# Eight minima over a row of zeros behind each tile, on VectorE, in a fused residual add and RMS norm

## The chip, the cores and the metric

The kernel runs on one core of a Trainium2 chip. The metric is the device time of one execution in microseconds (us). A ratio is the mean time of one kernel's runs over the mean of the other's runs of the same rounds, so it is not quite the ratio of the medians that are quoted.

## The reference

```python
z = x + residual                                   # 32 x 2048 x 2048, float32
rms = np.sqrt(np.mean(z ** 2, axis=-1, keepdims=True) + eps)
return (z / rms * gamma).astype(np.float32)
```

It reads 1074 MB and writes 537 MB.

## The kernel before

The 65536 rows are cut into 74 tiles, of 128 partitions times 7 rows but for the first two. Two buffers `z` hold x, then the sum, then the result. One area `r_area` of 11 rows holds the residual, with four rows to spare, so that a new residual can land while half of the old one is still read. SyncE issues the x loads and the stores on one queue, ScalarE issues the residual loads, but for the first two, on another.

```python
def sp_turn(sp, t):                      # SyncE, one tile
    t.wait(sp, "done", -1)
    # ... store of tile i-1, from z[(i-1) % 2]
    t.wait(sp, "s_out", -1)              # the store has landed: that z is free
    # ... load of x for tile i+1 into it (for the last tile in four parts)

def dve_turn(v, t, own):                 # VectorE, one tile
    t.wait(v, "x_in"); t.wait(v, "r_in")
    (a0, b0), (a1, b1) = parts(i)
    inc(add(v, i, a0, b0), "add_a", i)
    inc(add(v, i, a1, b1), "add_b", i)
    for h, (a, b) in enumerate(parts(i)):
        t.wait(v, "rms_a" if h == 0 else "rms_b")
        v.reciprocal(...)
        ins = scale(v, i, a, b, rstd[p][h])
    inc(ins, "done", i)

# ScalarE: waits for add_a, issues the residual load of tile i+1,
# then sums the squares of each half and takes the root
```

Of the kernel before, what the change touches and what calls it, by code (L numbers as in the profile page):

```python
# [9 lines left out]
def kernel(  # L10
# [5 lines left out]
    eps: float,  # L16
    out: bass.AP,
):



# [7 lines left out]
    P = nc.NUM_PARTITIONS  # L29
# [20 lines left out]
    last = n_tiles - 1  # L50

    LO = 3
# [12 lines left out]
    def sb(name, shape):  # L65
        return ctx.enter_context(nc.sbuf_tensor(name, shape, fp32))
# [6 lines left out]
    def sem(name):  # L73
        sems.append(ctx.enter_context(nc.semaphore(name)))
        return sems[-1]
# [6 lines left out]
    ssq = [[sb(f"ssq{p}{h}", [P, 4]) for h in range(2)] for p in range(2)]  # L82
    rms = [[sb(f"rms{p}{h}", [P, 4]) for h in range(2)] for p in range(2)]
    rstd = [[sb(f"rstd{p}{h}", [P, 4]) for h in range(2)] for p in range(2)]
    tail_ssq = sb("tail_ssq", [P, R])
    tail_rms = sb("tail_rms", [P, R])
    tail_rstd = sb("tail_rstd", [P, R])
# [8 lines left out]
    dve = sem("dve_own")  # L96
    act = sem("act_own")
    s_tail = sem("s_tail")
    tail_ev = {k: sem(f"tail_{k}") for k in ("add", "rms", "done")}


# [7 lines left out]
    def parts(i):  # L109
        if i == 0:  # L110
            return [(0, 2), (2, sizes[0])]
        k = sizes[i] if i < 2 else R
        return [(STEP, k), (0, STEP)] if i % 2 else [(0, R - STEP), (R - STEP, R)]
# [15 lines left out]
    def inc(ins, kind, i):  # L129
        return ins.then_inc(ev[kind][i % 2], U)  # L130
# [38 lines left out]
    def add(v, i, a, b):  # L169
        e = entry(i)  # L170
        s = z[i % 2][:, a:b, :]
        return v.tensor_add(out=s, in0=s, in1=r_area[:, e + a : e + b, :])  # L172

    def scale(v, i, a, b, rs, c=0):
        for g in range(a, b):
            s = z[i % 2][:, g, :]
            ins = v.scalar_tensor_tensor(  # L177
                out=s,
                in0=s,
                scalar=rs[:, c + g - a : c + g - a + 1],  # L180
                in1=gamma_tile[:, :],
                op0=mult,
                op1=mult,
            )
        return ins

    def dve_turn(v, t, own):
        i, p = t.i, t.p
        t.wait(v, "x_in")
        t.wait(v, "r_in")  # L190
# [4 lines that stand above are left out]
            n = b - a  # L195
            t.wait(v, "rms_a" if h == 0 else "rms_b")
            v.reciprocal(out=rstd[p][h][:, :n], in_=rms[p][h][:, :n]).then_inc(dve, U)  # L197
            v.wait_ge(dve, own(i, h))
            ins = scale(v, i, a, b, rstd[p][h])
        inc(ins, "done", i)  # L200


    class Chain:
# [69 lines left out]
    def vector_program(v):  # L273
        v.memset(eps_tile[:, :], float(eps))  # L274
        v.memset(stage, 0.0).then_inc(tail_ev["add"], 1)  # L275
        v.wait_ge(g_in, 4 * U)
        v.stream_shuffle(gamma_tile[:, :].rearrange("p (a b) -> p a b", a=16), stage, [0] * 32)  # L277
        for i in range(LO):
            dve_turn(v, Turn(i), lambda i, h: (2 * i + h + 1) * U)
        with v.Fori(0, 2 * n_iter, 2) as it:  # L280
            for i in range(LO, LO + 2):
                dve_turn(v, Turn(i, it), lambda i, h: it * (2 * U) + (2 * i + h + 1) * U)
        for i in range(HI, last):
            dve_turn(v, Turn(i), lambda i, h: (2 * i + h + 1) * U)
        base = 2 * last * U
        t = Turn(last)
        t.wait(v, "r_in")

        def tail_scale(k):
            a, b = tail[k]  # L290
            v.wait_ge(tail_ev["rms"], k + 1)
            v.reciprocal(out=tail_rstd[:, a:b], in_=tail_rms[:, a:b]).then_inc(dve, U)  # L292
            v.wait_ge(dve, base + (k + 1) * U)
            scale(v, last, a, b, tail_rstd, a).then_inc(tail_ev["done"], 1)

        for k, (a, b) in enumerate(tail):
            v.wait_ge(x_tail[k], U)
            add(v, last, a, b).then_inc(tail_ev["add"], 1)
            if k:
                tail_scale(k - 1)  # L300
        tail_scale(len(tail) - 1)
# [21 lines left out]

    sync_program(nc.sync)
    vector_program(nc.vector)
    scalar_program(nc.scalar)

# [40 lines left out]
```

## Time and profile before

| what | before |
|---|---|
| time, median of 3 | 3724.92 us |
| period of one tile | 50.8 us, 22.02 MB |
| transfers | 433 GB/s over the span |
| VectorE busy | 62% |
| VectorE waits for x | 1252.5 us, 17.6 us a tile |
| first add of the last tile waits for x | 5.6 us |

### The profile page before, as it was taken

The numbers are of one execution on the slowest core, as the hardware profiler recorded it, in microseconds if no ns is written. First come the engines' busy times: TensorE is split into PE (matmuls) and PEld (weight loads), VectorE is DVE, ScalarE is ACT, GpSimd is POOL, SyncE is SP. The second block draws the span as 40 slices with busy tenths as digits, with TensorE's granted clock in tenths as the row PEclk, the third lists the DMA queues.
The fourth block names the chain that finished last, engine by engine and source line by source line (L and its number), as shares of the span: only waits on it lengthen the run. The fifth ranks groups of instructions, "written<-read, shape, count | busy, mean of one in ns | idle before, by whom it ended". The sixth has DMA issues, their size and how long they took to land.

```text
span 3723.7 us, 3798 instructions
## 1 busy us (share of the span) xinstructions
DVE 2302.6 (62%) x816; ACT 1072.4 (29%) x1176; POOL 0.2 (0%) x4
## 2 busy tenths in 40 slices
DVE  5666665566665566665566665566665566665566
ACT  2233322233322233322233322233322233322233
POOL 0000000000000000000000000000000000000000
DMA  9999999999999999999999999999999999999999
GB/s 421 431 434 435 434 434 435 434 435 435 434 434 434 434 434 434 434 434 433 434 434 434 434 434 434 434 434 434 434 434 434 434 434 434 434 434 434 434 432 398
DMA packets 32963, 1610.68 MB, mean 433 GB/s; under 512 B 3712, under 2 KB 3776, under 8 KB 3776
## 3 DMA queue, kind: packets, MB, share of 16 engines
q1 hardware_dynamic: 22592, 1082.17, 67.2%
q10 hardware_dynamic: 10368, 528.49, 32.8%
q14 instruction: 3, 0.02, 0.0%
HBM read 1073.77 MB, written 536.87 MB: 433 GB/s over the span
## 4 chain that ended last, share of the span: by engine, by line
DMA 67%; DVE 22%; issue 9%; ACT 2%; SPq 0%; DVEq 0%; ACTq 0%
DMA out_dram<-z 39%; DMA z<-in_x_dram 27%; DVE z L172 15%; DVE z L177 7%; ACT sq_junk L223 1%; ACT rms L231 0%; DVE rstd L197 0%; SPq L259 0%; DVEq L127 0%; DVE r_area L275 0%; ACTq L211 0%; ACTq L127 0%; SPq L141 0%; DVE tail_rstd L292 0%; SPq L162 0%
## 5 line engine op out<-in xcount | busy, mean ns | idle before, releaser
L172 DVE TENSOR_TENSOR z<-z,r_area 128x8192 f32<-128x8192 f32 (+2 forms) x150 | 1109.5, 7437 | 1252.5 <-DMA z<-in_x_dram 1252.5
L223 ACT ACTIVATE sq_junk<-z 128x2048 f32<-128x2048 f32 x512 | 963.4, 1882 | 2617.1 <-DVE z L172 2605.7
L177 DVE SCALAR_TENSOR_TENSOR z<-z,rstd,gamma_tile 128x2048 f32<-128x2048 f32 x505 | 1153.6, 2344 | 5.2
L197 DVE RECIPROCAL rstd<-rms 128x4 f32<-128x4 f32 (+2 forms) x146 | 25.3, 173 | 130.8 <-ACT rms L231 130.8
L223 ACT ACTIVATION_READ_ACCUMULATOR sq_junk<-z 128x1 f32 x512 | 95.5, 186 | 0.0
L231 ACT ACTIVATE rms<-ssq,eps_tile 128x4 f32<-128x4 f32 (+2 forms) x146 | 43.3, 297 | 13.4
L177 DVE SCALAR_TENSOR_TENSOR z<-z,tail_rstd,gamma_tile 128x2048 f32<-128x2048 f32 x7 | 16.2, 2345 | 0.1
L277 DVE LOAD_MASK_SELECT gamma_tile<-r_area x1 | 0.0, 14 | 16.1 <-DMA r_area<-in_gamma_dram 16.1
L277 DVE STREAM_SHUFFLE gamma_tile<-r_area 128x2048 f32<-128x2048 f32 x1 | 2.3, 2290 | 0.0
L275 DVE MEMSET r_area<- 128x2048 f32 x1 | 1.8, 1765 | 0.4 <-issue 0.4
L223 ACT ACT_TABLE_LOAD x1 | 1.3, 1283 | 0.9 <-SPq L77 0.9
L231 ACT ACT_TABLE_LOAD x1 | 1.3, 1283 | 0.1
L231 ACT ACTIVATE tail_rms<-tail_ssq,eps_tile 128x2 f32<-128x2 f32 (+1 forms) x4 | 1.2, 295 | 0.1
L274 DVE MEMSET eps_tile<- 128x1 f32 x1 | 0.1, 59 | 1.0 <-SPq L77 1.0
L292 DVE RECIPROCAL tail_rstd<-tail_rms 128x2 f32<-128x2 f32 (+1 forms) x4 | 0.6, 158 | 0.0
L349 POOL MEMSET const-bfloat16-1.0<- 128x1 bf16 x1 | 0.1, 101 | 0.0
L349 POOL MEMSET const-uint8-127<- 128x1 uint8 x1 | 0.1, 101 | 0.0
L349 POOL MEMSET const-float32-0.0<- 128x1 f32 x1 | 0.1, 98 | 0.2 <-issue 0.2
L349 POOL MEMSET const-float32-1.0<- 128x1 f32 x1 | 0.1, 98 | 0.0
## 6 DMA issues: line engine op xcount, KB each, us to landing
r_area<-in_residual_dram ACTq DMA_DIRECT2D x72, 7168.0 KB, 35.5
z<-in_x_dram SPq DMA_DIRECT2D x71, 7168.0 KB, 27.5
out_dram<-z SPq DMA_DIRECT2D x71, 7168.0 KB, 40.8
z<-in_x_dram SPq DMA_DIRECT2D x3, 2048.0 KB, 17.9
out_dram<-z SPq DMA_DIRECT2D x3, 2048.0 KB, 15.0
r_area<-in_residual_dram SPq DMA_DIRECT2D x1, 5120.0 KB, 25.0
z<-in_x_dram SPq DMA_DIRECT2D x1, 5120.0 KB, 36.7
out_dram<-z SPq DMA_DIRECT2D x1, 5120.0 KB, 26.5
```

The source lines that it names most:

```text
L172: return v.tensor_add(out=s, in0=s, in1=r_area[:, e + a : e + b, :])
L177: ins = v.scalar_tensor_tensor(out=s, in0=s, scalar=rs[:, c + g - a : c + g - a + 1], in1=gamma_tile[:, :], op0=mult, op1=mult,)
L197: v.reciprocal(out=rstd[p][h][:, :n], in_=rms[p][h][:, :n]).then_inc(dve, U)
L223: s.activation(out=sq_junk[:, :], in_=src[:, g, :], func=Act.Square, accum_out=sq[:, g - a : g - a + 1],)
L231: return s.activation(out=rm, in_=sq[:, : b - a], func=Act.Sqrt, bias=eps_tile[:, :], scale=inv_d)
L274: v.memset(eps_tile[:, :], float(eps))
L275: v.memset(stage, 0.0).then_inc(tail_ev["add"], 1)
L277: v.stream_shuffle(gamma_tile[:, :].rearrange("p (a b) -> p a b", a=16), stage, [0] * 32)
L292: v.reciprocal(out=tail_rstd[:, a:b], in_=tail_rms[:, a:b]).then_inc(dve, U)
L349: nc = _bacc.Bacc("TRN2", target_bir_lowering=False, num_devices=1)
```

## The change

It adds VectorE work that nobody uses, behind the last scaling of each of the tiles 3 to 72, where VectorE would wait for the next x. No other engine's program changes. The intent is to see whether work in a wait costs anything.

```diff
+    zeros = sb("zeros", [P, 1536])
+    least = sb("least", [P, 8])
...
+    spare = sem("spare")
...  in dve_turn
         inc(ins, "done", i)
+        if i >= LO:
+            v.wait_ge(spare, i - LO + 1 if t.it is None else t.it + (i - LO + 1))
+            v.tensor_reduce(
+                out=least[:, :],
+                in_=zeros[:, :].unsqueeze(1).to_broadcast([P, 8, 1536]),
+                op=mybir.AluOpType.min,
+                axis=mybir.AxisListType.X,
+            ).then_inc(spare, 1)
...  in vector_program
         v.memset(stage, 0.0).then_inc(tail_ev["add"], 1)
+        v.memset(zeros[:, :], 0.0).then_inc(spare, 1)
         v.wait_ge(g_in, 4 * U)
...  ahead of the last tile
+        v.wait_ge(spare, last - LO + 1)
```

## The prediction

> **What bounds the kernel now.** I read the page from the top: engine shares, the slices, then the chain that ended last, then the waits, then one period of the timeline, and last the tail. First the page:
>
> ```profile
> span 3723.7 us, 3798 instructions
> DVE 2302.6 (62%) x816; ACT 1072.4 (29%) x1176; POOL 0.2 (0%) x4
> ...
> GB/s 421 431 434 435 434 434 435 434 435 435 434 434 434 434 434 434 434 434 433 434 434 434 434 434 434 434 434 434 434 434 434 434 434 434 434 434 434 434 432 398
> ...
> DMA 67%; DVE 22%; issue 9%; ACT 2%; SPq 0%; DVEq 0%; ACTq 0%
> ```
>
> VectorE is busy 62% of the span, and the transfers run at 433 to 435 GB/s in every slice but the first two and the last two. 1610.68 MB at 434 GB/s take 3711 us of the 3724: the kernel is bound by its transfers. Next, who waits for whom:
>
> ```profile
> ACT sq_junk L223 <- DVE z L172: 2605.7, 149, 35.3
> DVE z L172 <- DMA z<-in_x_dram: 1252.5, 74, 18.7
> DVE rstd L197 <- ACT rms L231: 130.8, 73, 6.2
> ```
>
> VectorE's big wait is for x. Asked for 150 to 3650 us alone, the same view gives 1216.8 us in 69 waits, 17.63 us each. The timeline shows where each lies:
>
> ```profile
> 1858.63 15.16 DVE L172 TENSOR_TENSOR z<-z,r_area 128x6144 f32<-128x6144 f32 x2 [17.63 <-DMA z<-in_x_dram]
> ...
> 1882.69 9.12 DVE L177 SCALAR_TENSOR_TENSOR z<-z,rstd,gamma_tile 128x2048 f32<-128x2048 f32 x4
> 1891.84 0.34 SPq L153 DMA_DIRECT2D out_dram<-z  x1
> 1909.43 15.16 DVE L172 TENSOR_TENSOR z<-z,r_area 128x6144 f32<-128x6144 f32 x2 [17.62 <-DMA z<-in_x_dram]
> ```
>
> One period is 1909.43 - 1858.63 = 50.80 us, and it moves three blocks of 7.34 MB (x, residual, out), 22.02 MB: 433 GB/s, so the period is the transfers' time. VectorE's work on a tile runs from 1858.63 to 1891.81 = 33.2 us; then it issues nothing until x lands. That gap is the room the change has. It is stable: in the timelines I read of the steady stretch it is 17.61 to 18.00 us, and 18.73 after tile 3, the first tile that gets the new work.
>
> The last tile is different, because its x comes in four parts:
>
> ```profile
> 3661.65 9.12 DVE L177 SCALAR_TENSOR_TENSOR z<-z,rstd,gamma_tile 128x2048 f32<-128x2048 f32 x4
> ...
> 3676.41 4.43 DVE L172 TENSOR_TENSOR z<-z,r_area 128x4096 f32<-128x4096 f32 x1 [5.63 <-DMA z<-in_x_dram]
> ...
> 3681.24 4.43 DVE L172 TENSOR_TENSOR z<-z,r_area 128x4096 f32<-128x4096 f32 x1 [0.40 <-DMA z<-in_x_dram]
> ...
> 3690.41 18.76 SPq L269 DMA_DIRECT2D out_dram<-z  x4
> ```
>
> Here the gap is 5.63 us, not 17.6, and from 3681 to 3708.8 VectorE works nearly without a pause. The last store is issued at 3708.84 and lands 13.8 us later by the list of transfers, about 1 us before the end.
>
> **What the Trainium skill says.** Four places.
> - "VectorE: DVE Perf Modes", section "The perf-mode tier table (the rule you actually need)": `tensor_reduce` runs at 1x in every dtype, one element per cycle, as fp32 `tensor_tensor` does, for which it gives 2293 ns at 2048 elements. The trace has 2287 ns for the add of that size, so the table fits for the add; no reduce is in this trace.
> - The same page, "Rules for kernel authors", calls `tensor_reduce` the slowest DVE op and says to expect 1x. Nothing here tests it; it is why I keep a rival with a slower reduce.
> - "SBUF — State Buffer", section "Who interferes with whom": transfers have ports of their own and never contend with a compute engine. The trace agrees (columns: stretch, length, busy VectorE, ScalarE and GpSimd, clock, transfer share, GB/s):
>
> ```profile
> 1841.00:1858.60 17.60, 0.00 (x0) 0.00 (x0) 0.00 (x0) 1.00 0.99 427
> 1858.60:1873.80 15.20, 15.17 (x3) 6.30 (x7) 0.00 (x0) 1.00 1.02 441
> 1873.80:1881.00 7.20, 6.94 (x4) 7.03 (x7) 0.00 (x0) 1.00 1.03 446
> ```
>
>   With VectorE idle the transfers move 427 GB/s, with it fully busy 441 and 446. Busy VectorE costs them nothing visible.
> - "DMA: Bandwidth & Descriptors", section "Where 436 GB/s comes from": the fabric in front of SBUF carries 435.2 GB/s. The slices show 433 to 435, so this kernel is at that ceiling, with no rate left to win or to catch up with.
>
> **The change, part by part.** It removes nothing.
>
> 1. One memset of 128x1536 zeros before the gamma shuffle. The memset of 128x2048 took 1765 ns, so about 1765 x 1536/2048 = 1.3 us. Right after it VectorE waits 16.07 us for gamma; hidden, 0 us. The memset whose end releases the gamma load still comes first.
>
> 2. In the loop over tiles 3 to 72, one reduce behind each tile: 70 of them, each one instruction over 8 x 1536 = 12288 elements. Its duration from the adds: 128x8192 takes 8685 ns, 128x4096 takes 4421 ns; the slope is 4264/4096 = 1.041 ns per element and the fixed part 8685 - 8192 x 1.041 = 157 ns. So 12288 x 1.041 + 157 = 12.95 us (estimate). All 70: 906 us more of VectorE, from 2302.6 to about 3210 us, 86% of the span.
>
> 3. Where it lies. The order of VectorE's instructions in the built program has the reduce behind the last scaling of a tile and ahead of the next tile's first add. The store of the tile is released by the scaling, which is ahead of the reduce, so it is issued as before. The reduce then starts at once and ends 12.95 us into a gap of 17.63 us; 17.63 - 12.95 = 4.7 us of wait remain. The add starts when x lands, as before. Cost per tile: 0, for 69 of the 70. The waits for x should fall by 69 x 12.95 = 894 us.
>
> 4. The wait on the new semaphore is for the reduce of one tile earlier, 50 us past; it and the register operation that goes with it cost some tens of ns inside the gap: 0.
>
> 5. The 70th reduce meets the short gap. It starts at 3670.8 and ends at 3683.75, so the first add of the last tile starts 7.4 us late. The second add would have started at 3681.24 and starts at about 3688.2: 7.0 us late, as 0.4 us of wait are used up. Everything after follows on VectorE without slack, so the four last stores are issued 7.0 us later, the last at 3715.8 instead of 3708.84. How much of 7.0 us reaches the end depends on the transfers still queued. In the kernel before they run near full rate until 3715 although the last store was issued at 3708.84: its 13.8 us to land are mostly queueing, since 1.05 MB take 2.4 us at 434 GB/s. After the change, the third store (2.1 MB) is issued at about 3713.3 to an almost empty queue. Its bytes and the last store's, 3.15 MB, take 7.3 us; for start and landing I take 2.9 us, which is what the first x load leaves (10.1 us for 3.15 MB, some of it shared): landing at 3713.3 + 7.3 + 2.9 = 3723.5, against 3722.6 before. So about +1 us, and surely less than +7; I take +2.5 us, as my queue model is crude.
>
> Sum: 0 + 0 + 69 x 0 + 2.5 = 2.5 us on 3724.9, giving **3727.5 us**.
>
> **The rivals.**
>
> A. The reduce is slower than an element per cycle. The room is 17.63 us, that is 36% over my estimate, or 1.42 ns per element. At two cycles per element it lasts 25.75 us, overruns by 8.1 us, and VectorE becomes the bound: 33.2 + 25.75 = 59 us a tile against 50.8, 70 x 8.1 = 570 us more, near 4295 us. For it: no reduce in this trace, the skill's remark on the slowest op, and an input with step 0 over the eight repeats. Against it: the tier table, and the inner 1536 elements are contiguous. I give it 6%.
>
> B. VectorE's reads slow the transfers. At even 2% less rate in the 12.95 us per tile this would cost 70 x 0.26 = 18 us. Against it: 427 GB/s idle and 441 busy, above. Under 3%.
>
> C. The busy share as the bound: adding 906 us to VectorE in full would give 4631 us. Against it: the gap in front of each first add ends with x, not with VectorE. Nearly excluded.
>
> D. The tail hands on its whole 7 us: 3732 us. Possible if the stores' landing doesn't shrink; still within 2%.
>
> E. A gain from reordered transfers: no store or load is issued earlier, so none. Under 1%.
>
> **Range and chances.** Between no loss and D lie 3724 and 3732 us; a little spare on both sides for chip noise (the three runs differ by 0.2 us) and for weak contention gives 3722 to 3738. Faster by over 2%: 0.01. Slower by over 2% needs more than 74 us, that is over 1 us a tile, which only A does: 0.07. Within 2%: 0.92.
>
> **What would show it.** Right: 70 reduces of about 12950 ns; VectorE near 3210 us and 86%; its wait for x down from 1252.5 to about 350 us, some 4.7 us a tile; period still 50.8 us; slices still at 434 GB/s; in the tail no wait ahead of the first add, the last store issued near 3715.8 and landing in about 8 us. Wrong: a reduce of over 17.6 us with no wait for x left (A), slices under 430 GB/s with waits left over (B), or a last store that still takes 13.8 us to land (D).

## The result, and the profile after

The changed kernel takes 3725.21 us (median of 4 runs, 3724.81 to 3725.66) against 3724.94 us of the kernel before (4 runs, 3724.76 to 3725.41). The ratio is 1.0001, 95% interval 0.9983 to 1.0018: the same time, with 906 us more work.

From the page of the changed kernel: the span, engine shares, GB/s by slice and the new group (line, engine, operation, output and input, count, then busy us, mean ns, idle before).

```profile
span 3723.9 us, 3939 instructions
DVE 3204.3 (86%) x887; ACT 1072.4 (29%) x1176; POOL 0.2 (0%) x4
...
GB/s 421 431 433 434 434 434 434 434 434 434 436 434 434 434 434 434 434 434 434 434 434 435 434 434 434 434 434 434 434 434 434 434 434 434 434 434 434 434 433 398
...
L207 DVE TENSOR_REDUCE least<-zeros 128x8 f32<-128x12288 f32 x70 | 906.3, 12947 | 0.0
```

VectorE went from 62% to 86% of the span and the slices did not move. The busy share alone tells nothing of the time. Who waited for whom in the changed kernel (total us, times, longest):

```profile
ACT sq_junk L235 <- DVE z L176: 2613.0, 148, 34.9
DVE z L176 <- DMA z<-in_x_dram: 359.0, 72, 13.4
DVE rstd L201 <- ACT rms L243: 130.8, 73, 6.2
```

Only the middle line changed, from 1252.5 to 359.0 us: the new work was taken out of the wait for x, 893.5 us of it, while ScalarE's waits are those of before. The timeline of the same stretch as before (start, duration):

```profile
1841.36 12.95 DVE L207 TENSOR_REDUCE least<-zeros 128x8 f32<-128x12288 f32 x1
1859.23 15.16 DVE L176 TENSOR_TENSOR z<-z,r_area 128x6144 f32<-128x6144 f32 x2 [4.92 <-DMA z<-in_x_dram]
...
1892.33 12.95 DVE L207 TENSOR_REDUCE least<-zeros 128x8 f32<-128x12288 f32 x1
1910.05 15.16 DVE L176 TENSOR_TENSOR z<-z,r_area 128x6144 f32<-128x6144 f32 x2 [4.77 <-DMA z<-in_x_dram]
```

The reduce starts as soon as the tile's scaling ends and is over 4.8 us before x lands; from add to add it is still 50.82 us. The tail of the changed kernel:

```profile
3670.80 12.95 DVE L207 TENSOR_REDUCE least<-zeros 128x8 f32<-128x12288 f32 x1
3683.79 8.76 DVE L176 TENSOR_TENSOR z<-z,r_area 128x4096 f32<-128x4096 f32 x2
...
3697.61 18.76 SPq L281 DMA_DIRECT2D out_dram<-z  x4
```

Here the reduce overran the short gap: the first add has no wait in front of it and starts at 3683.79 instead of 3676.41, and the last four stores are issued 7.2 us later (3697.61 against 3690.41 for the first). Yet the end moved by 0.2 us. The list of transfers (the last store, KB, us from issue to landing) says why; first the kernel before,

```profile
out_dram<-z SPq DMA_DIRECT2D x1, 1024.0 KB, 13.8
```

then the changed kernel:

```profile
out_dram<-z SPq DMA_DIRECT2D x1, 1024.0 KB, 6.7
```

The store is issued 7 us later and lands 7 us sooner after its issue: in the kernel before it had stood in a queue.

### The profile page after: what moved, and what is told of

Same layout as the page of the kernel before. It is cut to its first block, busy times and chain, and to the rows that moved or that the text cites. A ratio compares the mean times of both kernels' runs of the same rounds, so it can differ in the third digit from the quotient of the medians.

```text
span 3723.9 us, 3939 instructions
## 1 busy us (share of the span) xinstructions
DVE 3204.3 (86%) x887; ACT 1072.4 (29%) x1176; POOL 0.2 (0%) x4
## 4 chain that ended last, share of the span: by engine, by line
DMA 66%; DVE 23%; issue 9%; ACT 2%; DVEq 0%; SPq 0%; ACTq 0%
DMA out_dram<-z 39%; DMA z<-in_x_dram 27%; DVE z L176 15%; DVE z L181 7%; ACT sq_junk L235 2%; DMA r_area<-in_gamma_dram 0%; DVE least L207 0%; ACT rms L243 0%; DVE rstd L201 0%; DVEq L293 0%; DVEq L131 0%; SPq L271 0%; DVE r_area L287 0%; ACTq L223 0%; ACTq L131 0%
## 5 line engine op out<-in xcount | busy, mean ns | idle before, releaser
L176 DVE TENSOR_TENSOR z<-z,r_area 128x8192 f32<-128x8192 f32 (+2 forms) x150 | 1109.3, 7437 | 359.1 <-DMA z<-in_x_dram 359.0
L181 DVE SCALAR_TENSOR_TENSOR z<-z,rstd,gamma_tile 128x2048 f32<-128x2048 f32 x505 | 1153.6, 2344 | 5.2
L207 DVE TENSOR_REDUCE least<-zeros 128x8 f32<-128x12288 f32 x70 | 906.3, 12947 | 0.0
L201 DVE RECIPROCAL rstd<-rms 128x4 f32<-128x4 f32 (+2 forms) x146 | 25.3, 173 | 130.8 <-ACT rms L243 130.8
## 6 DMA issues: line engine op xcount, KB each, us to landing
z<-in_x_dram SPq DMA_DIRECT2D x71, 7168.0 KB, 27.5
out_dram<-z SPq DMA_DIRECT2D x71, 7168.0 KB, 40.8
```

What stands on the lines that cost most here:

```text
L176: return v.tensor_add(out=s, in0=s, in1=r_area[:, e + a : e + b, :])
L181: ins = v.scalar_tensor_tensor(out=s, in0=s, scalar=rs[:, c + g - a : c + g - a + 1], in1=gamma_tile[:, :], op0=mult, op1=mult,)
L201: v.reciprocal(out=rstd[p][h][:, :n], in_=rms[p][h][:, :n]).then_inc(dve, U)
L207: v.tensor_reduce(out=least[:, :], in_=zeros[:, :].unsqueeze(1).to_broadcast([P, 8, 1536]), op=mybir.AluOpType.min, axis=mybir.AxisListType.X,
```

## The experiments

The theory to test: **work is free in a place as long as it fits the room of that place.** The room is set by the next thing that has to happen there, for the change the landing of x, 17.6 us after the last scaling. The rivals: queued transfers absorb overruns too, so the gap is no sharp edge; VectorE's total per period is what counts, not the place; the chain of waits is to be read word for word, so anything ahead of a store costs its full length. I made twelve kernels; all gave correct outputs. Each ran four times, but those with sixteen repeats, the one in bf16 and the two of the tail, which ran twice. The kernel before ran beside each of them, and the ratios are to it.

### How much: 10, 11, 12 and 16 repeats

The edit, for n = 10, 11, 12, 16:

```diff
-    least = sb("least", [P, 8])
+    least = sb("least", [P, n])
-                in_=zeros[:, :].unsqueeze(1).to_broadcast([P, 8, 1536]),
+                in_=zeros[:, :].unsqueeze(1).to_broadcast([P, n, 1536]),
```

Expected for ten:

> Ten repeats instead of eight: 15360 elements, by the measured fixed part (12947 - 12288/0.96 = 147 ns) 15360/0.96 + 147 = 16147 ns. Room theory (free until the reduce fills the 17.6 us gap): ratio to before 1.000, about 1.5 us of wait for x left per tile, 3724 to 3728 us. Rival 'added work costs a share of its length': 2/8 more work than the change as made should move the time visibly; it would not be 1.000 again. Rival 'contention': slices under 433 GB/s.

For eleven:

> Eleven repeats: 16896/0.96 + 147 = 17747 ns, against a room of 50.82 - 33.14 = 17.68 us per tile. Room theory: the wait for x is gone from the loop and the time grows by 0.07 us x 69 = 5 us, plus up to 10 us in the tail, so 3726 to 3745 us: the edge. A transfer-slack rival (queued transfers absorb overruns of some us): exactly as before, also at twelve repeats.

For twelve:

> Twelve repeats: 18432/0.96 + 147 = 19347 ns, 1.67 us over the room. Room theory: VectorE is the bound, period 33.14 + 19.35 = 52.5 us, 69 x 1.67 = 115 us plus some 7 us in the tail, about 3847 us (ratio 1.033); no wait for x in the loop; transfers down to about 420 GB/s. Transfer-slack rival: ratio under 1.01, because the x is early anyway and queues absorb the delay.

For sixteen:

> Sixteen repeats: 24576/0.96 + 147 = 25747 ns, what rival A of the prediction assumed (two cycles per element). Room theory: period 33.14 + 25.75 = 58.9 us, 69 x 8.07 = 557 us plus some 14 us of tail, about 4296 us (ratio 1.153). Slope from rep12 to rep16 6.4 us x 70 = 448 us, one for one. Transfer-slack rival: less than one for one.

| repeats | one reduce, ns | period, us | time, us | ratio (95%) |
|---|---|---|---|---|
| 8 (the change) | 12947 | 50.82 | 3725.21 | 1.0001 (0.9983 to 1.0018) |
| 10 | 16147 | 50.83 | 3727.85 | 1.0008 (0.9991 to 1.0024) |
| 11 | 17747 | 50.83 | 3730.22 | 1.0013 (0.9997 to 1.0030) |
| 12 | 19347 | 52.35 | 3837.67 | 1.0303 (1.0285 to 1.0320) |
| 16 | 25747 | 58.75 | 4285.70 | 1.1505 (1.1482 to 1.1528) |

The durations are those expected to the nanosecond. The edge is sharp and lies between 17.75 and 19.35 us. With ten repeats the wait for x is 1.58 us a tile; with twelve it is gone from the loop, as its timeline shows, and the reduce runs into the add:

```profile
1838.93 19.35 DVE L207 TENSOR_REDUCE least<-zeros 128x12 f32<-128x18432 f32 x1
1858.19 15.15 DVE L176 TENSOR_TENSOR z<-z,r_area 128x6144 f32<-128x6144 f32 x2
...
1891.29 19.34 DVE L207 TENSOR_REDUCE least<-zeros 128x12 f32<-128x18432 f32 x1
```

Past the edge VectorE is the bound, and each further us costs a us: from 12 to 16 repeats 4285.70 - 3837.67 = 448.0 us, and 70 x (25.747 - 19.347) = 448.0 us. Nothing is absorbed in the loop, so the first rival falls at this place; the tail, below, does absorb something. My absolute figures for 12 and 16 repeats (3847 and 4296) were 10 us too high. The period is the reduce plus 33.00 us (52.35 - 19.35, 58.75 - 25.75), not plus 33.14: the new instruction and the add behind it each start a little before the recorded end of the one in front. The room is therefore 50.82 - 33.00 = 17.82 us, and eleven repeats just fit it.

### What: the same elements in bf16

```diff
-    zeros = sb("zeros", [P, 1536])
+    zeros = ctx.enter_context(nc.sbuf_tensor("zeros", [P, 1536], mybir.dt.bfloat16))
```

with sixteen repeats.

> Sixteen repeats on zeros kept as bf16, behind the tile: as many elements as in the run with sixteen repeats of fp32, half the bytes. If the reduce goes by elements (one per cycle in every dtype): 25747 ns each and about 4286 us, as there. If it goes by bytes: 12.95 us each and 3725 us.

The kernel took 4285.36 us, ratio 1.1504. From the groups of its page:

```profile
L207 DVE TENSOR_REDUCE least<-zeros 128x16 f32<-128x24576 bf16 x70 | 1802.2, 25746 | 0.0
```

25746 ns against 25747 in fp32: the reduce goes by elements. Two sizes in fp32 give (25747 - 12947)/12288 = 1.0417 ns for one element, one cycle of the 0.96 GHz that the Trainium skill's page "VectorE: DVE Perf Modes" gives in its section "Specifications", as its tier table has it, and a fixed 147 ns.

### The tail: 0 and 16 repeats behind the last full tile alone

The loop was made one round shorter, so that the turn of tile 72 stands alone, and its reduce was taken away (k = 0; the wait ahead of the last tile then asks for one reduce fewer) or doubled (k = 16):

```diff
-    n_iter = (last - LO) // 2
+    n_iter = (last - LO) // 2 - 1
...
-        if i >= LO:
+        k = 0 if i == last - 1 else 8        # or 16 if ...
+        if i >= LO and k:
...
-                in_=zeros[:, :].unsqueeze(1).to_broadcast([P, 8, 1536]),
+                in_=zeros[:, :].unsqueeze(1).to_broadcast([P, k, 1536]),
```

> Eight repeats everywhere, none behind the next to last tile. Tail theory: the tail is that of the kernel before: 5.6 us wait ahead of its first add, last store issued near 3708.9 and 13.8 us to land, span 3723.7; the time differs from the changed kernel's by under 1 us. If the reduce ahead of the tail cost something, this run is faster than the changed kernel by it.

> Eight repeats everywhere, but sixteen behind the next to last tile, the one in front of the short gap. Tail theory: the 7 us of delay of the change as made were swallowed by the queued transfers (last store 6.7 instead of 13.8 us to land), and that is used up; the reduce ends 12.8 us later than in the changed kernel, last store issued near 3728.8, landing again in about 6.7 us, span about 3736.7 us (+12.8 against the changed kernel, ratio 1.0034). Rival 'the tail has more slack': span under 3728.

Without that reduce: 3725.28 us, ratio 1.0000 (0.9980 to 1.0020), last store again 13.8 us to land. So the seven us by which the change delays VectorE in the tail cost nothing that can be measured. With sixteen: 3737.38 us, ratio 1.0032 (1.0012 to 1.0052), and the last store takes 6.3 us to land: 12.2 us more than the changed kernel for 12.8 us more reduce. (The changed kernel and the tail runs were timed in different rounds; the kernel before differs by 0.5 us between them.) The tail has a room of its own, 5.6 us of wait and some 7 us of queue, and eight repeats just fill it. That also agrees with the small rise at ten and eleven repeats, where the period did not move: their last reduce ends 3.2 and 4.8 us later than with eight, and they took 2.6 and 5.0 us more than the changed kernel.

### Where: ahead of the last scaling

The reduce with its eight repeats goes ahead of the second reciprocal, so that the store is issued later.

```diff
         t.wait(v, "rms_a" if h == 0 else "rms_b")
+        if h == 1:
+            reduce_zeros(v, t, i)            # the same lines as in the change
         v.reciprocal(...)
...
         inc(ins, "done", i)
-        (the reduce of the change)
```

> The same reduce, but ahead of the tile's second reciprocal and scaling (behind the wait for its rms), so the store of the tile is issued 12.95 us later. Chain reading (the chain that ended last runs through the scaling into the store, so what delays the scaling delays the end): 12.95 us per two tiles, 35 x 12.95 = 453 us, ratio 1.12. Queue reading (store and x load are on one queue, and the store stands behind the x load that lands 17.6 us after the store is issued): a store that is 12.95 us late still stands in the queue before its turn, ratio 1.000 to 1.003; store landing time down from 40.8 to about 28 us, reduce followed at once by work.

It took 3729.73 us, ratio 1.0010 (0.9994 to 1.0027). The chain of waits of the kernel before runs through this very scaling, on to the store, on to the next x; read word for word it promised 453 us. The timeline of this run (start, duration):

```profile
1846.79 9.12 DVE L181 SCALAR_TENSOR_TENSOR z<-z,rstd,gamma_tile 128x2048 f32<-128x2048 f32 x4
1855.94 0.34 SPq L157 DMA_DIRECT2D out_dram<-z  x1
1860.68 15.16 DVE L176 TENSOR_TENSOR z<-z,r_area 128x6144 f32<-128x6144 f32 x2 [4.77 <-issue]
```

And from its list of transfers, the stores (count, KB, median us to landing):

```profile
out_dram<-z SPq DMA_DIRECT2D x71, 7168.0 KB, 28.0
```

The view puts the wait of 4.77 us down to "issue"; by its issue at 1833.08 and 27.5 us to landing the x load lands at 1860.6, so it is still the wait for x. The store is issued 4.7 us before the next add instead of 17.6 us before it, and takes 28.0 us to land instead of 40.8. The 12.8 us between are queueing, for the x load ahead of it takes 27.5 us in both kernels. The third rival falls. In the kernel before the store stood behind the x load on SyncE's queue, as the Trainium skill's page "DMA: Bandwidth & Descriptors", section "Queues, rings and completion order", lets one expect: an engine takes the descriptors of one ring in ring order. A transfer's time to landing in a chain is thus work and queue together, and a delay that only shortens the queue costs nothing.

### Where: ahead of the first add

```diff
     t.wait(v, "x_in"); t.wait(v, "r_in")
+    reduce_zeros(v, t, i)
     (a0, b0), (a1, b1) = parts(i)
     inc(add(v, i, a0, b0), "add_a", i)
...
     inc(ins, "done", i)
-    (the reduce of the change)
```

> The same reduce, ahead of the tile's first add, after x landed: VectorE's sum per tile is the same 46.1 us, less than 50.8. Sum theory (only VectorE's total per period against the transfers' counts): ratio 1.000. Position theory: the add, and with it the next residual load that the add releases, come 12.95 us later; at the hand-over from store to next x load no residual is then in flight, so the transfers stand still 2 to 3 us per tile: 69 x 2.7 = about 186 us, ratio 1.03 to 1.06. Chain reading: 1.12.

It took 3981.86 us, ratio 1.0689 (1.0671 to 1.0707): 256 us more for the same VectorE work, in another place of the same tile. So VectorE's total is not what counts, and the second rival falls too. The size is over my range, and I had not foreseen the loop that the chain shows. The chain of waits of this run, one period:

```profile
1842.92 34.48 DMA r_area<-in_residual_dram
...
1877.58 12.95 DVE least L194
1890.53 6.48 DVE z L176
...
1897.17 34.59 DMA r_area<-in_residual_dram
```

And from its list of waits:

```profile
DVE least L194 <- DMA r_area<-in_residual_dram: 584.5, 69, 14.1
```

VectorE now waits for the residual, 8.5 us a tile. The chain no longer holds x or the store. The first add releases the next residual load, which releases the reduce, which delays the first add: 34.5 + 12.95 + 6.5 us and some issue time are the 54.25 us from one residual load to the next.

### Moved by one instruction: behind the first add

```diff
     inc(add(v, i, a0, b0), "add_a", i)
+    reduce_zeros(v, t, i)
     inc(add(v, i, a1, b1), "add_b", i)
...
     inc(ins, "done", i)
-    (the reduce of the change)
```

> The same reduce as in the run that has it ahead of the first add, moved by one instruction: behind the first add, which releases the next residual load, and ahead of the second add. Residual-loop theory (in the run with the reduce ahead of the first add the period was 34.6 us residual landing + 12.95 reduce + 6.5 first add + 0.2 = 54.25 us, a loop of its own, because that add releases the next residual load): the loop is broken, the period is 50.8 again, ratio 1.000 to 1.003; the store is 12.95 us late as in the run ahead of the last scaling. Rival (any work between x landing and the adds' end costs, since everything behind x landing is late): ratio near 1.07 again.

It took 3728.63 us, ratio 1.0017 (1.0000 to 1.0033); three of its four runs are at 3728.2 to 3728.8 and one at 3736.64. Nearly the whole 256 us hang on one instruction: the add whose end releases the residual load. The same add also lets ScalarE begin, but that is not where the time goes: VectorE's waits for ScalarE's root are 130.9 us in the run with the reduce ahead of the first add and 130.8 us in the kernel before.

### Ahead of the first add, shorter: 5 and 2 repeats

The run with the reduce ahead of the first add, with 5 and then 2 in place of 8.

> The reduce ahead of the first add with five repeats: 7680/0.96 + 147 = 8147 ns. Residual-loop theory: 35.5 + 8.15 + 6.5 + 0.2 = 50.35 us, under 50.8: no cost, ratio 1.000 to 1.004, room in this place 8.6 us. Rival (cost in proportion to the delay of the first add, 256 us x 8.15/12.95 = 161 us): ratio 1.043.

It took 3860.84 us, ratio 1.0367 (1.0350 to 1.0384). My expectation failed and the rival's (1.043) was nearer. The loop of the residual is not what bounds here: VectorE waits 11.5 us a tile for x in this run, and the x load takes 35.7 us to land instead of 27.5. I looked at the transfers in steps of 2 us (stretch, length, busy VectorE, ScalarE and GpSimd, clock, transfer share, GB/s). Data moves in packets, here nearly all of 57344 bytes, and the view counts a packet whole in the step in which it starts. Sixteen of them, one on each DMA engine, make 459 GB/s and a share of 1.06, so each lasts 1.06 x 2 = 2.12 us, longer than a step. A step with few bytes is therefore not yet a stop; rate and share have to be read together:

```profile
1814.00:1816.00 2.00, 0.00 (x0) 0.00 (x0) 0.00 (x0) 1.00 1.27 373
1816.00:1818.00 2.00, 0.00 (x0) 0.00 (x0) 0.00 (x0) 1.00 0.27 86
1818.00:1820.00 2.00, 0.21 (x1) 0.00 (x0) 0.00 (x0) 1.00 1.06 459
...
1834.00:1836.00 2.00, 2.00 (x2) 1.02 (x1) 0.00 (x0) 1.00 1.25 401
1836.00:1838.00 2.00, 2.00 (x1) 1.97 (x3) 0.00 (x0) 1.00 0.25 86
1838.00:1840.00 2.00, 2.00 (x1) 1.97 (x3) 0.00 (x0) 1.00 1.06 459
```

Twice a tile a round of packets lasts longer. The 13 packets that start between 1814 and 1816 have a share of 1.27, so 1.27 x 2 x 16/13 = 3.1 us each, and the three of the next step 2.9 us, against 2.12 us. This round lies near the end of the x load (VectorE sees x at 1819.79), with the store issued 7 us before; the other lies at the hand-over, where the store ends (1836.66) and the next x load is issued. In the kernel before, no step of the period that I looked at is under 344. Over the steady stretch, the kernel before, five repeats and eight repeats:

```profile
300.00:3400.00 3100.00, 1917.46 (x672) 892.71 (x977) 0.00 (x0) 1.00 1.00 434
300.00:3400.00 3100.00, 2319.81 (x707) 862.21 (x944) 0.00 (x0) 1.00 1.00 418
300.00:3400.00 3100.00, 2521.65 (x684) 833.00 (x912) 0.00 (x0) 1.00 0.97 404
```

With five repeats the DMA engines are as busy as before, at a lower rate: the time goes into longer packets, and 50.82 x 434/418 = 52.8 us is the period of that run. With eight repeats the share falls too, so there the transfers also stand still for a part of the time. At the hand-over the timeline suggests a reason: with five repeats the residual load is issued at 1834.59, 2 us before the store lands, and the long packets there are its first ones (16 on its queue, 2.8 us each); in the kernel before it is issued at 1814.55, 16.5 us before the store lands, and is well under way in the hand-over. That gave the last run:

> The reduce ahead of the first add with two repeats: 3072/0.96 + 147 = 3347 ns. Hand-over theory (what costs is a residual load that comes so late that nothing of it is in flight when the store ends and the next x load starts; with five repeats it was issued 2 us before the store landed, in the kernel before 16.5 us): with a delay of 3.35 us it is still issued some 13 us before, so no cost, ratio 1.000 to 1.002. Proportional rival (256 us for 12.95 us, 136 us for 8.15 us, so each us of delay of the first add costs 17 to 20 us): 136 x 3.35 / 8.15 = 56 us, ratio 1.015.

Three of its four runs took 3725.01, 3725.31 and 3726.35 us, as before; the fourth took 3764.30. The ratio is 1.0036 (0.9983 to 1.0090), which that one run puts outside my 1.000 to 1.002. The median of 3725.83 us and the profiled run (3725.01, transfers at 431 to 435 GB/s in all slices but the first two and the last two) are with the hand-over theory and against the proportional one, which wanted 56 us in each run, a ratio of 1.015. One run of four being 39 us longer stays unexplained.

So the room ahead of the first add is over 3.35 us, by three runs of four, and under 8.15 us, against 17.8 us behind the last scaling. That a hand-over without residual is what costs agrees with these two sizes, but no run takes it apart, and it is not shown. Why the packets last longer stays open, and so does the first of the two places, where the store is already issued. There the residual load has just landed too (issued at 1781.96, 34.5 us to landing); but in the kernel before x also hands over to the store, near 1858, with the residual landed since 1850, and the steps there have 430 GB/s. No residual in flight is thus not enough by itself.

No run was faster than the kernel before, and none could be expected to be: all these edits add work, and the transfers already run at 433 GB/s.

## Why the prediction was right

It gave 3727.5 us with a range of 3722 to 3738, and 0.92 for within 2%.

1. The memset: 1.3 us expected, 1.338 us measured, taken out of the wait for gamma (16.07 to 14.53 us). Right.
2. The reduce: 12.95 us expected, 12944 to 12948 ns measured in all 70. Right; the step that carried the most doubt, and the page's tier table was enough for it. VectorE's busy time came out at 3204.3 us, not 3210: the reduce starts some 0.08 us before the recorded end of the scaling, 70 times, and overlap counts once.
3. Its place: 4.7 us of wait left expected, 329.1 us in 69 waits = 4.77 us measured between 150 and 3650 us. The total wait for x is 359.0 us, with about 350 expected. Right, and the sweep of repeats shows that it is the gap that makes it free, not some slack elsewhere.
4. The wait for the semaphore: nothing to see. Right.
5. The tail: first add 7.4 us late (7.34 by its own figures) and last store at 3715.8 expected, 7.38 us and 3716.0 measured; landing in about 8 us expected, 6.7 measured. The end moved 0.2 us in the span. Here I took 2.5 us where my own queue reckoning said 1; the term was too large, by some 2 us. The tail runs show that the mechanism is the right one, and that there was no room left after it: 12.8 us more reduce cost 12.2 us.

The rivals: A, a slower reduce, was wrong as to the duration, but its price was right: 25.75 us per reduce was expected to give near 4295 us and gave 4285.70. B, slower transfers, is refused by the slices: 433 to 436 GB/s with VectorE at 86%, in all but the first two and the last. C, the busy share, is refused by the result. D expected the whole 7 us at the end and saw none of it.

What the prediction left out is that the wait for x was not the only room. It said that the store is issued as before, which was true and not needed: the run ahead of the last scaling delayed the store by 12.95 us and lost under 0.3% at the interval's upper end.

## What to carry to other kernels

Ask of added work not how large it is against an engine's idle share, but what the engine would have waited for in that very place, and how long; up to there it is free, and past it, in the loop here, each us cost a us. Ask too what the instruction behind it releases: the same 12.95 us cost nothing ahead of an add that releases nothing urgent, and 256 us ahead of the add that releases a load. And look at the last tile by itself, since its gaps differ from the loop's.

## What the Trainium skill lacked or had wrong

- "VectorE: DVE Perf Modes", "The perf-mode tier table (the rule you actually need)", gives `tensor_reduce` as 1x without a duration. Measured here: elements/0.96 GHz + 147 ns from 12288 to 24576 elements a partition (and 8154 ns, 7 more than that, for 7680 ahead of the first add, 3353 ns for 3072), the same in bf16 (25746 ns) as in fp32 (25747 ns), with an input whose outer step is 0.
- The same page, "Rules for kernel authors", calls it the slowest DVE op. Per element it costs what an fp32 add costs (1.04 ns); the fp32 `scalar_tensor_tensor` of this kernel took 2344 ns for 2048 elements, where 2048/0.96 + 147 = 2280 ns would be a reduce's (an estimate from the sizes measured; none of 2048 was run).
- "DMA: Bandwidth & Descriptors", "Where 436 GB/s comes from", says that for transfers between HBM and SBUF the HBM side binds at about 358 GB/s. Taken alone, that sentence does not hold here: one core, reading and writing HBM at once, held 433 GB/s over 3.7 ms. The page is not wrong as a whole, for its table of measured loads has a core alone at 425 GB/s; the sentence lacks that condition.
- The same page's "Queues, rings and completion order" has the order within a ring, but beyond the fixed cost of one DMA no page tells what it costs when several loads end and begin together: with five repeats ahead of the first add, rounds of packets of about 3 us instead of 2.12 us twice a tile, and 418 GB/s instead of 434.
